# ScalarE in place of VectorE for the two 32-wide casts to bf16 in each expert retrieval

## The chip, the core and the metric

The kernel runs on one core of a Trainium2 chip. The metric is the device time of one execution in microseconds, the median of the runs. TensorE (PE in the rows) multiplies matrices, VectorE is DVE, ScalarE is ACT, GpSimd is POOL and SyncE, which issues most loads, is SP. Each engine works through its own queue in order and waits on semaphores for the others.

## What is computed

One decoder layer over 256 tokens of width 2048: an input projection, a pooling mixer beside sparse attention, an output projection and a layer norm, then the part that matters here, a product-key retrieval over 128 x 128 = 16384 experts with one hidden neuron each, and a second layer norm.

```python
qh = (xc @ wq).reshape(PEER_CHUNK, PEER_HEADS, 2, PEER_HALF)
s1 = jnp.einsum('thd,kd->thk', qh[:, :, 0], sub_keys[0])
s2 = jnp.einsum('thd,kd->thk', qh[:, :, 1], sub_keys[1])
v1, i1 = lax.top_k(s1, PEER_TOPK)          # 16 of 128
v2, i2 = lax.top_k(s2, PEER_TOPK)
cand = (v1[..., :, None] + v2[..., None, :]).reshape(PEER_CHUNK, PEER_HEADS, PEER_TOPK * PEER_TOPK)
cidx = (i1[..., :, None] * PEER_KEYS + i2[..., None, :]).reshape(...)
best, pos = lax.top_k(cand, PEER_TOPK)     # 16 of 256
expert = jnp.take_along_axis(cidx, pos, axis=-1)
gate = jax.nn.softmax(best, axis=-1)
act = jax.nn.gelu(jnp.einsum('td,thkd->thk', xc, u[expert]), approximate=False)
return jnp.einsum('thk,thkd->td', (gate * act), v[expert])
```

## The kernel before

Weights come in units of 128x512 float32 (256 KB). For each unit `load_unit` issues a load into a `raw` buffer (four of them), and `split` makes two halves: `hi` on ScalarE, a cast to the rounded float32 type (L94), and `lo` on VectorE, the difference `raw - hi` (L95), for some units on GpSimd. There are four `hi` and four `lo` buffers. TensorE takes three products for each pair of tiles: hi x hi (L119), lo x hi (L120), hi x lo (L121). So a unit goes through SyncE, ScalarE, VectorE or GpSimd, and TensorE, and a buffer comes free when the last reader is done.

The part around the change has two streams that are woven together. One is the query projection `wq` (48 units here, besides 16 that were loaded early): its result is split into `qhh` and `qhl`, and multiplied with the subkeys into scores `sps`, both halves of a head and both tiles of 128 tokens. Behind it the products `ups` follow, 128 steps of 11 tiles, with units that were loaded ahead into free parts of the large tile `S` (L531). The units u_d are split by the same lines.

The other stream is `retrieve`: 8 heads times 2 token tiles, 16 calls. Each takes the 16 largest of 128 scores for both halves (`top16`: two maxima, two index searches, a replacement on VectorE; `v16` values, `x16` indices). GpSimd adds all pairs into `cand` (L564), VectorE takes the 16 largest of these 256 (`best`, `pos`), takes `pos` apart into `ab` (L571, L572), and compares with 0..15 into the one-hot `hot` (L577). GpSimd multiplies `hot` with the indices (L579), adds up (L582, L583), and VectorE writes the expert number `e_idx` (L584). The two casts of the change stand here: `xb`, the indices `x16` as bf16, which GpSimd's L579 reads, and `abb`, the `ab` pair as bf16, which L577 reads. Both are 128x32.

From `e_idx` GpSimd gathers expert rows with an indirect DMA, `g<-u_g` (L659), which VectorE multiplies and sums (L684). These are spread over the 128 `ups` steps. Then weights are extracted and scattered per token, and the same is done with the `v` table (`vacc`, L805, L813).

The order on each engine is set when the program is built: a scheduler that works with estimated times places the instructions, with a higher priority for what belongs to weight units (`tc.high_priority`). A changed engine can therefore move other instructions too.

Of the kernel before, what the change touches and what calls it, by code (L numbers as in the profile page):

```python
# [71 lines left out]
def layer(ctx, tc, A, out):  # L72
    nc = tc.nc
# [474 lines left out]
    def top16(vals, work, vout, iout):  # L548
        nc.vector.max(vout[:, 0:8], vals)
        nc.vector.max_index(iout[:, 0:8], vout[:, 0:8], vals)  # L550
        nc.vector.match_replace(work, vout[:, 0:8], vals, GONE)
        nc.vector.max(vout[:, 8:16], work)
        nc.vector.max_index(iout[:, 8:16], vout[:, 8:16], work)

    def retrieve(h, tt, sps):
        v16 = wqp.tile([P, 2, PK], F32, name="v16")
        x16 = wqp.tile([P, 2, PK], U32, name="x16")
        for half in range(2):
            vals = sps[:, half * P:(half + 1) * P]
            top16(vals, vals, v16[:, half], x16[:, half])  # L560
        xb = wqp.tile([P, 2, PK], BF16, name="xb", bufs=2)
        nc.vector.tensor_copy(xb, x16)
        cand = wqp.tile([P, PK, PK], F32, name="cand")
        nc.gpsimd.tensor_tensor(cand, v16[:, 0].unsqueeze(2).broadcast_to([P, PK, PK]),  # L564
                                v16[:, 1].unsqueeze(1).broadcast_to([P, PK, PK]), op=ALU.add)
        cflat = cand.rearrange("p a b -> p (a b)")
        pos = wqp.tile([P, PK], U32, name="pos")
        hs_ = slice(h * PK, (h + 1) * PK)
        top16(cflat, cflat, best[:, tt, hs_], pos)
        ab = wqp.tile([P, 2, PK], U32, name="ab")  # L570
        nc.vector.tensor_single_scalar(ab[:, 0], pos, 4, op=ALU.logical_shift_right)  # L571
        nc.vector.tensor_single_scalar(ab[:, 1], pos, 15, op=ALU.bitwise_and)  # L572
        abb = wqp.tile([P, 2, PK], BF16, name="abb", bufs=2)
        nc.vector.tensor_copy(abb, ab)
        hot = wqp.tile([P, PK, 2, PK], BF16, name="hot")
        flat = hot.rearrange("p k a j -> p k (a j)")
        nc.vector.tensor_tensor(hot, iota16.unsqueeze(2).broadcast_to([P, PK, 2, PK]),  # L577
                                abb.unsqueeze(1).broadcast_to([P, PK, 2, PK]), op=ALU.is_equal)
        nc.gpsimd.tensor_tensor(hot, hot, xb.rearrange("p a k -> p k a").unsqueeze(3).broadcast_to([P, PK, 2, PK]),  # L579
                                op=ALU.mult)  # L580
        for n in (8, 4, 2):
            nc.gpsimd.tensor_tensor(flat[:, :n], flat[:, :n], flat[:, n:2 * n], op=ALU.add)  # L582
        nc.gpsimd.tensor_tensor(i12[:, tt, :, hs_], hot[:, 0], hot[:, 1], op=ALU.add)  # L583
        nc.vector.scalar_tensor_tensor(e_idx[:, tt, hs_], i12[:, tt, 0, hs_], float(P), i12[:, tt, 1, hs_],  # L584
                                       op0=ALU.mult, op1=ALU.add)
# [10 lines left out]
    for h in range(HEADS):  # L596
        for half in range(2):
            with tc.high_priority(offset=AHEAD):
                if 2 * h + half < EARLY:
                    ps = first[2 * h + half]  # L600
                else:
                    ps = bankA("wq")[:, :T]
                    rows_T(ps, A["w_q"][2 * h + half], lambda kt: hs[kt])
                for f in late:
                    f()
                qh = tuple(wqp.tile([P, T], F32R, name=f"qh{s}", bufs=2) for s in "hl")
                split(qh[0], qh[1], ps)
            late = [lambda h=h, half=half, qh=qh: scores(h, half, qh)]
        if h == HEADS - 1:
            with tc.high_priority(offset=AHEAD):  # L610
                late[0]()
        if h > 0:
            for tt in range(NT):
                retrieve(h - 1, tt, sps[h - 1][:, tt])
    for tt in range(NT):
        retrieve(HEADS - 1, tt, sps[HEADS - 1][:, tt])
# [337 lines left out]
```

## Time and profile before

| | |
|---|---|
| median of 3 runs | 1751.63 us (1749.29 to 1753.16) |
| profiled execution | 1756.99 us, span from first to last instruction 1755.2 us |
| TensorE busy, granted clock | 1666.4 us (95%), 0.984 |
| VectorE busy | 1450.0 us (83%) |
| ScalarE busy | 897.5 us (51%) |
| GpSimd busy | 886.7 us (51%) |

The busy shares are means over stages that differ. The retrievals lie between 400 and 560 us of the span; the `ups` steps go on to about 1020 us, the extraction to about 1160, and the products with `v` to the end. A row of the trace gives the start of an instruction, its length, and in brackets the idle time of the engine ahead of it with what ended it.

### The profile page before, as it was taken

What the parts mean: (1) busy time and instruction counts of PE and PEld (TensorE: products, weight loads), DVE (VectorE), ACT (ScalarE), POOL (GpSimd) and SP (SyncE); (2) the same over time, 40 slices, a digit from 0 to 9 for tenths busy, and PEclk for the clock granted to TensorE, in tenths of its full rate; (3) what the DMA queues carried; (4) which work ended last, traced back from release to release, by engine and by line L of the source; (5) the groups of instructions that cost most, each with busy time, mean ns of one, the idle gap of its engine ahead of it and who ended that gap; (6) DMA issues with size and microseconds to landing.
All of it is one profiled execution on the core that took longest, in us unless ns stands there. A gap on an engine that the chain in (4) does not pass through costs nothing. (4 is left out here: it accounts for less than half of the span.)

```text
span 1755.2 us, 33099 instructions
## 1 busy us (share of the span) xinstructions
PE 1666.4 (95%) x10652; PEld 1484.7 (85%) x10652; DVE 1450.0 (83%) x3515; ACT 897.5 (51%) x1885; POOL 886.7 (51%) x899
## 2 busy tenths in 40 slices
PE   8999999989899999999999889988999999999996
PEld 8999888869888999999999788876687888888883
DVE  6766676679999888889888798877888888889896
ACT  6545565444344555555554358773454555555551
POOL 0000000036775656566565588856747645456562
PEclk9999999989999999999999999998999999999998
DMA  7667657726688999999999841137999999999962
GB/s 219 179 188 192 203 175 261 255 79 214 193 287 268 337 361 321 323 347 336 344 330 329 293 146 55 55 103 255 296 329 333 381 338 332 338 319 328 352 200 89
DMA packets 206014, 451.13 MB, mean 257 GB/s; under 512 B 26928, under 2 KB 31472, under 8 KB 205328
## 3 DMA queue, kind: packets, MB, share of 16 engines
q1 hardware_dynamic: 164816, 297.93, 51.4%
q0 software_dynamic: 41024, 151.09, 24.7%
q8 instruction: 84, 1.38, 0.3%
q14 instruction: 90, 0.74, 0.1%
HBM read 444.59 MB, written 4.26 MB: 256 GB/s over the span
## 5 line engine op out<-in xcount | busy, mean ns | idle before, releaser
L94 ACT CAST hi<-S 128x512 fp32r<-128x512 f32 x677 | 420.4, 622 | 450.5 <-PE vacc L121 223.2
L95 DVE TENSOR_TENSOR lo<-S,hi 128x512 fp32r<-128x512 f32 x672 | 464.5, 701 | 89.6 <-ACT hi L94 81.4
L121 PE MATMUL ups<-hTh,lo 128*128 128x256 f32 x1408 | 392.2, 283 | 11.7 <-DVE lo L95 11.1
L119 PE MATMUL ups<-hTh,hi 128*128 128x256 f32 x1408 | 392.2, 280 | 4.5 <-ACT hi L94 4.2
L120 PE MATMUL ups<-hTl,hi 128*128 128x256 f32 x1408 | 394.0, 281 | 0.0
L659 POOL DMA_INDIRECT g<-u_g,e_idx x256 | 289.2, 1130 | 173.1 <-DVE g L684 119.4
L94 ACT CAST hi<-raw 128x512 fp32r<-128x512 f32 x327 | 202.0, 621 | 245.4 <-PE projT L120 58.9
L95 DVE TENSOR_TENSOR lo<-raw,hi 128x512 fp32r<-128x512 f32 x303 | 216.6, 720 | 111.3 <-ACT hi L94 107.2
L120 PE MATMUL vacc<-lo,wt 128*128 128x512 f32 x744 | 278.4, 401 | 8.6 <-DVE lo L95 8.5
L121 PEld LDWEIGHTS ups<-hTh,lo 128*128 128x128 f32 x1408 | 263.5, 189 | 16.8 <-DVE lo L95 15.6
L121 PE MATMUL vacc<-hi,wt 128*128 128x512 f32 x744 | 276.2, 399 | 0.0
L119 PEld LDWEIGHTS ups<-hTh,hi 128*128 128x128 f32 x1408 | 266.0, 189 | 6.1 <-ACT hi L94 6.1
L120 PEld LDWEIGHTS ups<-hTl,hi 128*128 128x128 f32 x1408 | 265.7, 189 | 0.0
L119 PE MATMUL vacc<-hi,wt 128*128 128x512 f32 x744 | 231.2, 400 | 7.3 <-ACT wt L94 6.9
L805 POOL DMA_INDIRECT g<-v_g,e_idx x139 | 166.3, 1196 | 128.4 <-DVE accg L813 109.0
L684 DVE SCALAR_TENSOR_TENSOR g<-g,h_gath 128x640 f32<-128x640 f32 x256 | 204.9, 820 | 16.6 <-DMA g<-u_g,e_idx 16.1
L805 POOL DMA_INDIRECT raw<-v_g,e_idx x117 | 137.2, 1173 | 84.7 <-DVE accg L813 65.2
L120 PEld LDWEIGHTS vacc<-lo,wt 128*128 128x128 f32 x744 | 141.1, 190 | 45.7 <-DVE lo L95 12.0
L119 PEld LDWEIGHTS vacc<-hi,wt 128*128 128x128 f32 x744 | 141.2, 190 | 42.9 <-ACT wt L94 8.0
L121 PEld LDWEIGHTS vacc<-hi,wt 128*128 128x128 f32 x744 | 140.9, 189 | 34.5 <-issue 0.5
L714 POOL TENSOR_SCALAR bt<-cst,slotT 128x128 f32<-128x128 f32 x192 | 126.3, 675 | 23.3 <-POOL bt L714 16.4
L294 POOL TENSOR_TENSOR bias<-bias,score 128x128 f32<-128x128 f32 (+1 forms) x16 | 11.5, 739 | 233.1 <-DMA bias<-relb 115.8
(243 smaller groups left out, 3074.1 us busy)
## 6 DMA issues: line engine op xcount, KB each, us to landing
S<-v_d SPq DMA_DIRECT2D x361, 256.0 KB, 5.1
S<-u_d SPq DMA_DIRECT2D x328, 256.0 KB, 5.3
raw<-w_t SPq DMA_DIRECT2D x100, 256.0 KB, 2.8
raw<-w_n SPq DMA_DIRECT2D x64, 256.0 KB, 2.8
raw<-w_o SPq DMA_DIRECT2D x64, 256.0 KB, 3.3
raw<-w_q SPq DMA_DIRECT2D x48, 256.0 KB, 3.1
bc<-i_dram SPq DMA_DIRECT2D x32, 256.0 KB, 3.1
raw<-u_d SPq DMA_DIRECT2D x24, 256.0 KB, 5.1
```

The costliest lines, as they stand in the source:

```text
L94: last_copy[0] = nc.scalar.copy(hi, src).ins
L95: last_split[0] = (eng or nc.vector).tensor_tensor(lo, src, hi.bitcast(F32), op=ALU.subtract).ins
L119: mm(o, l[0], r[0], start=first, stop=False)
L120: mm(o, l[0], r[1], start=False, stop=False)
L121: return mm(o, l[1], r[0], start=False, stop=last).ins
L294: nc.gpsimd.tensor_tensor(bias[:, tt, :n], bias[:, tt, :n], sel[:, tt, :n], op=ALU.add)
L659: nc.gpsimd.indirect_dma_start(out=g, out_offset=None, in_=table, in_offset=bass.IndirectOffsetOnAxis(ap=e_idx[:, tt, slot:slot + 1], axis=0))
L684: nc.vector.scalar_tensor_tensor(g, g, 1.0, h_gath[:, tt], op0=ALU.mult, op1=ALU.mult, accum_out=pd[:, tt, slot:slot + 1])
L714: eng.tensor_scalar(bt[j][:, i], iota, i2T[:, t:t + 1], None, op0=ALU.is_equal)
L805: nc.gpsimd.indirect_dma_start(out=g, out_offset=None, in_=A["v_g"], in_offset=bass.IndirectOffsetOnAxis(ap=e_idx[:, tt, slot:slot + 1], a ...
```

## The change

Both casts of `retrieve` are issued on ScalarE. Nothing else in the text differs.

```diff
         xb = wqp.tile([P, 2, PK], BF16, name="xb", bufs=2)
-        nc.vector.tensor_copy(xb, x16)
+        nc.scalar.copy(xb, x16)
...
         abb = wqp.tile([P, 2, PK], BF16, name="abb", bufs=2)
-        nc.vector.tensor_copy(abb, ab)
+        nc.scalar.copy(abb, ab)
```

The scheduler also places other instructions of this stage anew; in front of it and from the middle of the `ups` steps on, the order is as it was. The sixth of the 16 retrievals shows it. On VectorE, from its `ab` pair on (the numbers tell tiles of one name apart; 5528, 5531 and 5533 belong to this retrieval, `xb_5724`, `cand_5726` and `v16_5747` to the next ones), before and then now:

```order
L571 TENSOR_SCALAR ab_5528<-pos_5522 128x16
L572 TENSOR_SCALAR ab_5528<-pos_5522 128x16
L552 MAX v16_5712<-sps_5460 128x8
L574 CAST abb_5531<-ab_5528 128x32
L553 MAX_INDEX x16_5713<-v16_5712,sps_5460 128x8
L577 TENSOR_TENSOR hot_5533<-iota16_4951,abb_5531 128x512
L562 CAST xb_5724<-x16_5713 128x32
L95 TENSOR_TENSOR lo_6027<-raw_6024,hi_6026 128x512
L549 MAX best_73<-cand_5726 128x8
L549 MAX v16_5747<-sps_5460 128x8
```

```order
L571 TENSOR_SCALAR ab_5528<-pos_5522 128x16
L572 TENSOR_SCALAR ab_5528<-pos_5522 128x16
L552 MAX v16_5712<-sps_5460 128x8
L553 MAX_INDEX x16_5713<-v16_5712,sps_5460 128x8
L584 SCALAR_TENSOR_TENSOR e_idx_72<-i12_74 128x16
L577 TENSOR_TENSOR hot_5533<-iota16_4951,abb_5531 128x512
L549 MAX best_73<-cand_5726 128x8
L549 MAX v16_5747<-sps_5460 128x8
L550 MAX_INDEX pos_5728<-best_73,cand_5726 128x8
L550 MAX_INDEX x16_5748<-v16_5747,sps_5460 128x8
L551 MATCH_REPLACE sps_5460<-v16_5747,sps_5460 128x128
L95 TENSOR_TENSOR lo_6027<-raw_6024,hi_6026 128x512
```

The two casts are gone, `e_idx` of an earlier retrieval stands ahead of `hot`, and `lo_6027` has moved behind two maxima, two index searches and a replacement. On ScalarE, at the same place, before and now:

```order
L94 CAST hi_5907<-raw_5905 128x512
L94 CAST hi_5926<-raw_5924 128x512
L94 CAST hi_6026<-raw_6024 128x512
L94 CAST qhh_5863<-wq_5782 128x256
L94 CAST hi_6045<-raw_6043 128x512
L94 CAST hi_6063<-raw_6061 128x512
L94 CAST hi_6082<-raw_6080 128x512
```

```order
L94 CAST hi_5907<-raw_5905 128x512
L574 CAST abb_5531<-ab_5528 128x32
L94 CAST hi_5926<-raw_5924 128x512
L562 CAST xb_5724<-x16_5713 128x32
L94 CAST hi_6026<-raw_6024 128x512
L94 CAST qhh_5863<-wq_5782 128x256
L94 CAST hi_6045<-raw_6043 128x512
L94 CAST hi_6063<-raw_6061 128x512
L574 CAST abb_5737<-ab_5734 128x32
L94 CAST hi_6082<-raw_6080 128x512
```

The `hi` casts keep their order among themselves, and `hi_5926`, `hi_6026` and `hi_6082` now stand behind casts that wait for VectorE. On GpSimd, at the same place, before and now:

```order
L564 TENSOR_TENSOR cand_5726<-v16_5712 128x256
L95 TENSOR_TENSOR lo_5927<-raw_5924,hi_5926 128x512
L579 TENSOR_TENSOR hot_5533<-hot_5533,xb_5518 128x512
L95 TENSOR_TENSOR lo_6046<-raw_6043,hi_6045 128x512
L582 TENSOR_TENSOR hot_5533<-hot_5533 128x256
```

```order
L564 TENSOR_TENSOR cand_5726<-v16_5712 128x256
L579 TENSOR_TENSOR hot_5533<-hot_5533,xb_5518 128x512
L95 TENSOR_TENSOR lo_5927<-raw_5924,hi_5926 128x512
L582 TENSOR_TENSOR hot_5533<-hot_5533 128x256
L95 TENSOR_TENSOR lo_6046<-raw_6043,hi_6045 128x512
```

Both `lo` of GpSimd have moved one place back, behind a step of the one-hot work.

## Rows read from the trace of the kernel before

**Rows 1.** The page: busy time, share of the span and instructions of each engine.
```profile
PE 1666.4 (95%) x10652; PEld 1484.7 (85%) x10652; DVE 1450.0 (83%) x3515; ACT 897.5 (51%) x1885; POOL 886.7 (51%) x899
```
**Rows 2.** Busy time by stage; columns as in the first line.
```profile
core 0: us, PE busy (x) PEld busy (x) DVE busy (x) ACT busy (x) POOL busy (x), PEclk, DMA share, GB/s
400.00:480.00 80.00, 73.31 (x587) 71.88 (x586) 77.98 (x301) 29.21 (x54) 57.93 (x68) 0.96 0.64 206
480.00:560.00 80.00, 72.64 (x577) 69.68 (x575) 78.60 (x271) 36.34 (x69) 54.35 (x67) 0.98 0.83 275
...
580.00:960.00 380.00, 380.00 (x3227) 379.84 (x3226) 332.53 (x691) 196.44 (x364) 237.81 (x210) 1.00 0.96 338
```
**Rows 3.** Waits of TensorE, 400 to 580 us: total, times, longest.
```profile
PE ups L121 <- DVE lo L95: 6.3, 9, 2.6
PE wq L121 <- DVE lo L95: 5.3, 5, 1.9
```
**Rows 4.** Groups by shape on VectorE, 400 to 570 us: busy us, mean ns.
```profile
L562 DVE CAST xb<-x 128x32 bf16<-128x32 uint32 x16 | 12.1, 754 | 0.1
...
L553 DVE FIND_INDEX8 x<-v,sps 128x8 uint32<-128x128 f32 x32 | 9.1, 284 | 0.0
...
L574 DVE CAST abb<-ab 128x32 bf16<-128x32 uint32 x16 | 4.3, 272 | 0.0
```
**Rows 5.** VectorE in order of time, sixth retrieval: start us, length us.
```profile
455.10 0.16 DVE L572 TENSOR_SCALAR ab<-pos 128x16 uint32<-128x16 uint32 x1
455.18 0.29 DVE L552 MAX8 v<-sps 128x8 f32<-128x128 f32 x1
455.39 0.16 DVE L574 CAST abb<-ab 128x32 bf16<-128x32 uint32 x1
...
455.78 0.66 DVE L577 TENSOR_TENSOR hot<-iota,abb 128x512 bf16<-128x512 bf16 x1
456.37 1.26 DVE L562 CAST xb<-x 128x32 bf16<-128x32 uint32 x1
```
**Rows 6.** GpSimd in order of time, the same place.
```profile
456.12 1.47 POOL L95 TENSOR_TENSOR lo<-raw,hi 128x512 fp32r<-128x512 f32 x1
```
**Rows 7.** VectorE in order of time, first retrieval.
```profile
406.48 0.16 DVE L562 CAST xb<-x 128x32 bf16<-128x32 uint32 x1
406.55 0.28 DVE L549 MAX8 v<-sps 128x8 f32<-128x128 f32 x1
```
**Rows 8.** Groups by shape on ScalarE, first the whole span, then 400 to 570 us.
```profile
L733 ACT ACTIVATE val<-val 128x8 f32<-128x8 f32 x32 | 6.4, 200 | 8.1 <-DVE val L732 8.1
...
L629 ACT ACTIVATE best<-best 128x128 f32<-128x128 f32 x2 | 0.6, 312 | 3.0 <-DVE best L627 3.0
```
**Rows 9.** ScalarE in order of time: `hi` at the first, eighth and last retrieval.
```profile
411.93 0.62 ACT L94 CAST hi<-raw 128x512 fp32r<-128x512 f32 x1 [0.22 <-DVE sps L551]
...
468.50 0.62 ACT L94 CAST hi<-raw 128x512 fp32r<-128x512 f32 x1 [2.62 <-PE wq L120]
...
544.91 0.62 ACT L94 CAST hi<-S 128x512 fp32r<-128x512 f32 x1 [0.78 <-DMA S<-u_d]
```
**Rows 10.** VectorE: end of the `ab` pair in these three, and the last `e_idx`.
```profile
413.05 0.16 DVE L572 TENSOR_SCALAR ab<-pos 128x16 uint32<-128x16 uint32 x1
...
473.57 0.16 DVE L572 TENSOR_SCALAR ab<-pos 128x16 uint32<-128x16 uint32 x1
...
550.17 0.17 DVE L572 TENSOR_SCALAR ab<-pos 128x16 uint32<-128x16 uint32 x1
...
556.24 0.17 DVE L584 SCALAR_TENSOR_TENSOR e_idx<-i 128x16 int32<-128x16 f32 x1 [1.03 <-POOL i L583]
```
**Rows 11.** Waits of ScalarE, 400 to 560 us.
```profile
ACT hi L94 <- DMA raw<-w_q: 27.7, 17, 3.7
```

## The prediction

> **What bounds the kernel now.** I began with the busy shares of the page: TensorE is busy for 95% of the span, VectorE for 83%, ScalarE for 51% [rows 1]. A change on VectorE and ScalarE can therefore only pay where TensorE is not the limit, so the next view is the busy time by stage. The retrievals fall into 400 to 560 us. There the reader should see two things. First, VectorE is full: 77.98 and 78.60 us of two stretches of 80 us. Second, TensorE does 587 and 577 matrix products in them, 1164 in 160 us, while from 580 to 960 us it does 3227 in 380 us and is never idle [rows 2]. At that later pace, 380/3227 = 0.118 us each, 1164 products need 137 us. So TensorE loses about 23 us in this stage, and at 580 us it is back at full pace with nothing made up. The third view says on whom it waits: on the `lo` halves of the weights that VectorE subtracts, 6.3 + 5.3 = 11.6 us of idle time in 14 waits [rows 3]. (Idle time is less than lost time here, because matrix products that come late also come thinly spaced.) The stage is VectorE's, and a microsecond freed there can reach TensorE, up to some 12 to 23 us. What follows is TensorE at full pace to 960 us, so a shift at 560 us travels on to there. I expect it to travel to the end, because every later load and gather is released by work in step with TensorE.
>
> **What the change removes.** The two casts take 12.1 us (16 `xb`, mean 754 ns) and 4.3 us (16 `abb`, mean 272 ns) of VectorE [rows 4], together 16.4 us. Not all of that is freed. A short instruction overlaps its neighbour: the `ab` shift at 455.10 is followed by the next start at 455.18, and the `xb` at 406.48 by a start at 406.55 [rows 5, 7]. So an undisturbed cast, 0.16 us long, holds up the queue for 0.08 us. Thirty-two of them free 32 x 0.08 = 2.6 us for certain. The rest of the 16.4 us is 16.4 - 32 x 0.16 = 11.3 us by which casts are stretched. Where that comes from is seen in one place: `xb` starts at 456.37 and lasts 1.26 us, until 457.63 [rows 5], while GpSimd runs its `lo` from 456.12 to 457.59 [rows 6]. The cast stands until GpSimd's instruction is over. `FIND_INDEX8` meets the same GpSimd work and has the same length everywhere, 284 ns in the mean of 32 [rows 4], so not every VectorE instruction is held like this.
>
> How much of the 11.3 us is really saved depends on who comes next. In the new order the instructions behind `hot` are two maxima, two index searches and a replacement, and only then a `lo`. The searches are not held. But GpSimd was busy for 57.93 us of 80 [rows 2], so the next instruction that can be held (`lo`, `hot`, the `ab` pair, `e_idx`) will often meet another GpSimd instruction. Also, the GpSimd `lo` that `xb` used to wait for now stands behind GpSimd's `hot`, so it falls closer to VectorE's own `lo`. The bounds are nothing saved and all saved. Nothing in the trace tells which is nearer, and I take half, 5.7 us. VectorE is then freed of 2.6 + 5.7 = 8.3 us, with bounds of 2.6 and 13.9.
>
> **What it adds.** ScalarE gets 32 casts of 128x32. The trace has none there. The nearest rows are an activation of 128x8 at 200 ns and one of 128x128 at 312 ns [rows 8]; I take 0.22 us, nearest the first, and 32 x 0.22 = 7 us on an engine that is busy for 29.21 us of 80 [rows 2]. That time alone costs nothing.
>
> The hand-over can cost. `hot` on VectorE needs `abb`. In the old order one maximum and one index search stood around the cast; in the new order they stand between the `ab` pair and `hot`, sometimes with `e_idx` or a `lo` as well. From the end of the pair (455.26) to the start of `hot` (455.78) that is about 0.5 us, the cast's own share of 0.1 included [rows 5], so 0.4 us of cover against 0.22. If ScalarE is free when the pair ends, `hot` does not wait. If a `hi` cast has just begun, 0.62 us long [rows 9], the hop takes up to 0.84 and `hot` waits up to 0.4 us. With ScalarE busy for a third of the time, this is about 16 x 0.33 x 0.2 = 1 us in all. I charge 1 us, with bounds of 0 and 16 x 0.4 = 6.4.
>
> The `xb` that is cast at this point serves GpSimd's product of the next retrieval (5533 is multiplied with `xb_5518`, cast one retrieval earlier), about 9 us later, so its hop costs nothing. Without that lead GpSimd would wait some 0.3 us each time, and it has 22 us of idle time in 80.
>
> The queue behind the casts is the second thing. ScalarE works in order, and its `hi` casts ran ahead of VectorE. Where a `hi` starts before the `ab` pair is done, the cast in front of it now makes it wait. I went through the 16 places, taking the end of the second `ab` [rows 10] less the start of the ScalarE instruction that will stand behind `abb` [rows 9]. The first is 413.21 - 411.93 = 1.3 us, the eighth 473.73 - 468.50 = 5.2, the last 550.34 - 544.91 = 5.4; two are nothing, and the 16 add up to 42 us. Most of this should not be felt: four `hi` buffers lie between ScalarE and TensorE, these `hi` halves then waited for their `lo` anyway, and VectorE comes to the pair sooner than it did. I take nothing, and price the other case below.
>
> The sum: 8.3 - 1 = 7.3 us freed on VectorE, less than the 11.6 and the 23 us that TensorE can take up, and some of TensorE's thin spacing should go too, which I round up to **8 us**. The profiled execution took 1756.99 us around its span of 1755.2; the sum makes it 1749. The median of the unprofiled runs is 5.4 us lower, 1751.63, and becomes **1743.6**.
>
> A page speaks against this. The Trainium skill, in "VectorE: DVE Perf Modes", section on the TRN2 errata, has a table of fixed costs in which a copy of 32 elements between SBUF places is (58 + 32)/0.96 GHz = 94 ns on VectorE and (224 + 32)/1.2 GHz = 213 ns on ScalarE. "ScalarE: Activation LUTs", in its rules for kernel authors, gives simple arithmetic to VectorE. By that table alone 32 casts get 3.8 us dearer and the estimate would be 1755.4. The undisturbed casts of this trace agree in kind (0.16 us long, 0.08 in the queue), but the mean of `xb` is 754 ns.
>
> **The rivals.**
> *The cast was cheap, and the wait moves on.* If the next VectorE instruction stands behind the same GpSimd work each time, only the 2.6 us of the short casts are freed, and `hot`'s hand-over takes as much (16 x 0.16 us, something between my 1 us and the bound of 6.4). The sum is 0, and the time 1751.6. For it: GpSimd's 72% busy share, and `lo` moved to where it meets VectorE's `lo`. Against it: two or more unheld instructions stand behind `hot` now. This is how the Trainium skill's table would come true.
> *ScalarE falls into step with VectorE.* The place is a `hi` held behind `abb` or `xb`, whose `lo` GpSimd makes: its raw buffer comes free late, the next `w_q` load starts late, and ScalarE already waits 27.7 us for these loads [rows 11]. A retrieval takes (550.34 - 413.21)/15 = 9.14 us, and TensorE needs 4 units of 12 products and 6 score products, 54 x 0.118 = 6.4 us. The point from which it decides is thus a hold of 2.7 us. Seven of the 16 holds are longer, by 12.3 us together. All of that lost, against 8 gained, is +4.3, and the time 1755.9. Against it: the holds are counted from VectorE's old, late times, and late ones belong to `lo` halves that VectorE now makes behind the pair anyway.
>
> **How the numbers follow.** The forecast has 0.63; its own range comes from VectorE's bounds, -(13.9 - 0) to -(2.6 + 0.3 x 11.3 - 2), where a third of the stretching is saved and 2 us are lost at `hot`: 1737.7 to 1747.6. "The wait moves on" has 0.20, because the busy GpSimd is a real obstacle. The slower rival has 0.17. About 0.2% (3.5 us) is what a measurement here can tell from no change. All of the forecast but 0.05 is faster by more than that, and 0.02 of the first rival: 0.60. Of the second rival 0.13 is slower by more, and 0.03 of the first: 0.16. The rest is 0.24. The range 1736 to 1756 takes in the forecast's own range and both rivals' times, and leaves out about 0.13: what goes beyond my best case for VectorE, and holds that cost more than counted.
>
> **What would show it.** Right: between 400 and 560 us the TensorE count rises well above 1164 and the idle time before `lo` falls below 11.6 us; the last `e_idx` of the retrievals comes 6 to 10 us sooner than 556.24 [rows 10]; VectorE's `lo` and `ab` means rise, but by less than 11.3 us in all; 580 to 960 us looks the same, earlier. Wrong in the first way: `lo`, `ab` and `hot` take up the whole stretching. Wrong in the second: ScalarE's idle time before `hi` is ended by VectorE, TensorE waits for GpSimd's `lo`, and w_q loads land late. A gain at 560 us that is gone at 1020 would refute the step that a shift travels on, and a GpSimd or ScalarE wait at `hot` above 2 us the charge for the hand-over.

## The result, and the profile after

The changed kernel took 1744.86 us, the median of 11 runs (1736.69 to 1746.80). The kernel before took 1751.79 us in 11 runs on the same chip (1748.54 to 1757.03). The recorded ratio of the two sets of runs is 0.995, with a 95% interval of 0.9937 to 0.9962. The medians differ by 6.9 us, which by itself is a ratio of 0.996. The change is faster, by about 0.4 to 0.5%. The forecast was 1743.6.

The profiled execution of after took 1739.89 us, its span 1738.1. That is among the fastest of its 11 runs, while the profile of before was at the slow end of its own. The two profiles differ by 17.1 us and the medians by 6.9, so the profiles are compared here by what happens inside the stage of the retrievals, and the totals by medians. The first part of the page, to be held against [rows 1]:

```profile
PE 1657.5 (95%) x10652; PEld 1477.1 (85%) x10652; DVE 1434.8 (83%) x3483; ACT 899.2 (52%) x1917; POOL 884.1 (51%) x899
```

VectorE has 32 instructions and 15.2 us less, ScalarE 32 instructions more. The busy time by stage of after, columns as in [rows 2]:

```profile
400.00:480.00 80.00, 74.36 (x605) 72.62 (x604) 76.59 (x308) 31.73 (x75) 63.90 (x74) 0.98 0.71 222
480.00:560.00 80.00, 75.54 (x615) 72.64 (x614) 75.95 (x250) 39.51 (x87) 59.71 (x69) 1.00 0.86 286
560.00:580.00 20.00, 19.93 (x168) 19.76 (x169) 18.38 (x40) 9.98 (x19) 13.49 (x13) 1.00 0.91 306
580.00:960.00 380.00, 378.68 (x3245) 378.48 (x3245) 333.58 (x696) 198.00 (x369) 233.97 (x209) 1.00 0.96 339
```

TensorE does 605 + 615 = 1220 products between 400 and 560 us, 56 more than the 1164 of before. With the next 20 us, where before had 155, it is 1388 against 1319. Those 69 products are 69 x 0.118 = 8.1 us of TensorE's later pace. From 580 to 960 us the pace is as it was. VectorE is no longer quite full: 76.59 and 75.95 us against 77.98 and 78.60.

TensorE's waits from 400 to 580 us (total, times, longest), against [rows 3], and the last `e_idx`, against [rows 10]:

```profile
PE wq L121 <- DVE lo L95: 4.7, 4, 1.7
PE ups L121 <- DVE lo L95: 3.0, 6, 1.0
...
547.84 0.18 DVE L584 SCALAR_TENSOR_TENSOR e_idx<-i 128x16 int32<-128x16 f32 x1 [1.03 <-POOL i L583]
```

The idle time before `lo` falls from 11.6 to 7.7 us, and the retrievals end at 547.84 where they ended at 556.24: 8.4 us sooner.

Those 3.9 us of idle time are half of the 8.1 us that TensorE won. Much of the rest is its clock, which the sections above leave out. These rows of before show TensorE at the end of a wait, then a stretch that follows and the one behind it (columns as in [rows 2]):

```profile
467.14 0.39 PE L121 MATMUL wq<-hTh,lo 128*128 128x256 f32 x1 [1.90 <-DVE lo L95]
...
468.50:471.90 3.40, 3.40 (x18) 3.40 (x17) 3.40 (x13) 1.51 (x3) 2.57 (x5) 0.50 0.62 222
471.90:475.30 3.40, 3.40 (x31) 3.40 (x30) 3.40 (x19) 1.24 (x2) 0.62 (x1) 1.00 0.70 217
```

TensorE is busy throughout both. At a granted clock of 0.50 (1.2 GHz) it does 18 products in 3.4 us, at 1.00 (2.4 GHz) it does 31. Before has three stretches of 3.4 us at 0.50 between 400 and 560 us (from 444.6, 468.5 and 492.4), after has one (from 473.0). Each of the four begins at the end of one of TensorE's longest waits in this stage, or up to 1.4 us later (1.84, 1.90 and 2.63 us long in before, 1.63 in after); another wait of 1.67 us in after is not followed by one. Two stretches less are, as an estimate from these rows, 2 x 13 = 26 products, or 26 x 0.118 = 3.1 us.

**Where VectorE got the time from.** These are VectorE's other groups by shape from 400 to 560 us, busy us and mean ns of one. First before, which the sections above did not show:

```profile
L95 DVE TENSOR_TENSOR lo<-S,hi 128x512 fp32r<-128x512 f32 x36 | 27.8, 774 | 0.0
L95 DVE TENSOR_TENSOR lo<-raw,hi 128x512 fp32r<-128x512 f32 x22 | 20.6, 937 | 0.3 <-ACT hi L94 0.3
L577 DVE TENSOR_TENSOR hot<-iota,abb 128x512 bf16<-128x512 bf16 x16 | 7.8, 489 | 0.0
L571 DVE TENSOR_SCALAR ab<-pos 128x16 uint32<-128x16 uint32 x16 | 7.6, 472 | 0.0
L572 DVE TENSOR_SCALAR ab<-pos 128x16 uint32<-128x16 uint32 x16 | 4.3, 271 | 0.0
L584 DVE SCALAR_TENSOR_TENSOR e_idx<-i 128x16 int32<-128x16 f32 x16 | 4.0, 250 | 1.0 <-POOL i L583 1.0
```

And after:

```profile
L95 DVE TENSOR_TENSOR lo<-S,hi 128x512 fp32r<-128x512 f32 x41 | 34.7, 853 | 0.5 <-ACT hi L94 0.4
L95 DVE TENSOR_TENSOR lo<-raw,hi 128x512 fp32r<-128x512 f32 x23 | 20.5, 891 | 1.5 <-ACT hi L94 1.5
L577 DVE TENSOR_TENSOR hot<-iota,abb 128x512 bf16<-128x512 bf16 x16 | 8.2, 514 | 0.1
L584 DVE SCALAR_TENSOR_TENSOR e_idx<-i 128x16 int32<-128x16 f32 x16 | 8.0, 502 | 2.3 <-POOL i L583 2.2
L571 DVE TENSOR_SCALAR ab<-pos 128x16 uint32<-128x16 uint32 x16 | 3.1, 197 | 0.0
L572 DVE TENSOR_SCALAR ab<-pos 128x16 uint32<-128x16 uint32 x16 | 2.7, 171 | 0.0
```

I take lengths near the shortest of the trace as undisturbed (`lo` 0.67 us, `hot` 0.41, the small ones 0.16) and call what a mean lies above that, times its count, the stretching. Before, with the casts of [rows 4], it is 30.4 us; after, 20.5. The casts' own 11.3 us are gone. The `ab` pair lost 6.0 us of stretching too, which nobody had asked for. `e_idx` took up 4.0 us, `lo` 3.0, `hot` 0.4: -11.3 - 6.0 + 4.0 + 3.0 + 0.4 = -9.9. Add 2.6 us for the 32 short casts, and 12.5 us are freed. VectorE's idle time in these 160 us rose from 3.4 to 7.5 us, so 12.5 - 4.1 = 8.4 us should show at the end of the stage. That the last `e_idx` shows just this is partly luck. The window of after holds some work of the next stage, and its retrievals began later (first maximum at 402.70 us, in before at 401.75). From the first maximum to the end of the last `e_idx` the stage is 154.7 us long before and 145.3 after, 9.3 us shorter. VectorE's waits of after (400 to 580 us) name the new idle time. None of them is at `hot`:

```profile
DVE e_idx L584 <- POOL i L583: 2.2, 3, 1.0
DVE lo L95 <- ACT hi L94: 2.1, 5, 1.1
...
DVE best L549 <- POOL cand L564: 1.2, 4, 0.5
```

Before, these were 1.0, 0.3 and 0.2 us.

**The sixth retrieval again.** VectorE, then GpSimd, then ScalarE in order of time (start, length), after, against [rows 5, 6]:

```profile
452.81 0.16 DVE L572 TENSOR_SCALAR ab<-pos 128x16 uint32<-128x16 uint32 x1
...
453.49 0.41 DVE L584 SCALAR_TENSOR_TENSOR e_idx<-i 128x16 int32<-128x16 f32 x1
453.83 0.41 DVE L577 TENSOR_TENSOR hot<-iota,abb 128x512 bf16<-128x512 bf16 x1
...
455.61 1.65 DVE L95 TENSOR_TENSOR lo<-raw,hi 128x512 fp32r<-128x512 f32 x1
```
```profile
453.25 0.62 POOL L564 TENSOR_TENSOR cand<-v 128x256 f32<-128x256 f32 x1
...
455.44 1.26 POOL L95 TENSOR_TENSOR lo<-raw,hi 128x512 fp32r<-128x512 f32 x1
```
```profile
453.01 0.22 ACT L574 CAST abb<-ab 128x32 bf16<-128x32 uint32 x1 [4.22 <-DVE ab L572]
453.13 0.61 ACT L94 CAST hi<-raw 128x512 fp32r<-128x512 f32 x1
453.67 0.22 ACT L562 CAST xb<-x 128x32 bf16<-128x32 uint32 x1
```

ScalarE's cast ends at 453.23, 0.6 us before `hot` starts: the hand-over is hidden. `hot` lasts 0.41 us where it lasted 0.66. The price has moved to two others. `e_idx` stands from 453.49 to 453.90, until GpSimd's `cand` (to 453.87) is over. `lo` meets GpSimd's `lo`, which ends at 456.70, and takes 1.65 us where one alone takes 0.67: it ends at 457.26, 0.56 us after GpSimd's.

### The profile page after: what moved, and what is told of

It reads as the page before. It is cut to its first block, busy times and chain, and to the rows that moved or that the text cites. A ratio compares the mean times of both kernels' runs of the same rounds, so it can differ in the third digit from the quotient of the medians.

```text
span 1738.1 us, 33114 instructions
## 1 busy us (share of the span) xinstructions
PE 1657.5 (95%) x10652; PEld 1477.1 (85%) x10652; DVE 1434.8 (83%) x3483; ACT 899.2 (52%) x1917; POOL 884.1 (51%) x899
## 5 line engine op out<-in xcount | busy, mean ns | idle before, releaser
L659 POOL DMA_INDIRECT g<-u_g,e_idx x256 | 284.8, 1112 | 171.4 <-DVE g L684 124.2
L805 POOL DMA_INDIRECT g<-v_g,e_idx x139 | 161.3, 1161 | 127.0 <-DVE accg L813 107.2
```

Source lines behind the costliest of these rows:

```text
L659: nc.gpsimd.indirect_dma_start(out=g, out_offset=None, in_=table, in_offset=bass.IndirectOffsetOnAxis(ap=e_idx[:, tt, slot:slot + 1], axis=0))
L805: nc.gpsimd.indirect_dma_start(out=g, out_offset=None, in_=A["v_g"], in_offset=bass.IndirectOffsetOnAxis(ap=e_idx[:, tt, slot:slot + 1], a ...
```

## The experiments

Three batches ran, each beside runs of before on the same chip; the medians of before there were 1765.68 us (30 runs), 1761.62 (23) and 1751.82 (35). Only ratios are therefore compared across batches. The first batch splits the change.

**One cast alone.** `xb_only` moves only L562, `abb_only` only L574.

```diff
-        nc.vector.tensor_copy(xb, x16)
+        nc.scalar.copy(xb, x16)
```

> Only xb is cast on ScalarE; abb stays on VectorE. Theory A (VectorE is freed of what the casts hold up its queue, mostly the time in which they are stretched beside GpSimd): xb carries about 10.8 of the 13.8 us, so the last e_idx of the retrievals, at 556.24 us before and 547.84 with both casts moved, comes near 549.7, and the time is about 5 us below before. Theory B (the scheduler's new order of the other instructions makes the gain, whichever cast is moved): one cast moved gives as much as two or as little as none, without regard to its share. Theory C (the cast was cheap, the wait passes to the next VectorE instruction): the means of lo, ab and e_idx on VectorE rise by what xb gave up, and the time is within 2 us of before.

Measured: 1761.75 us, ratio 0.998 (0.9966 to 0.9994), last `e_idx` at 551.2, 1207 products from 400 to 560 us. That is between what theory A and theory C gave, and near A. Its order of the later stages changed as well, so its total is a weaker witness than its stage. And behind the stage, from 566.5 to 573.3 us, TensorE's granted clock is 0.50: by 580 us it has done 1317 products, no more than before's 1319.

```diff
-        nc.vector.tensor_copy(abb, ab)
+        nc.scalar.copy(abb, ab)
```

> Only abb is cast on ScalarE; xb stays on VectorE. Theory A: abb carries 1.3 us of queue time and 1.8 us of stretching, less the hop in front of hot, so the last e_idx comes near 554.5 and the time is 0 to 2 us below before; xb on VectorE keeps a mean near 750 ns. Theory B: as large a gain as with both, 7 us. Theory C: no change, and hot waits for ScalarE.

Measured: 1756.55 us, ratio 0.9957 (0.994 to 0.9975), last `e_idx` at 549.5, 1215 products. Groups of VectorE, 400 to 560 us:

```profile
L562 DVE CAST xb<-x 128x32 bf16<-128x32 uint32 x16 | 7.9, 492 | 0.2
...
L572 DVE TENSOR_SCALAR ab<-pos 128x16 uint32<-128x16 uint32 x16 | 5.5, 343 | 0.0
```

The cast that was 1.8 us of stretching brings the stage's end 6.7 us forward, most of the gain. Theory A had asked for 554.5 and an `xb` near 750 ns, so it failed here, and the result is near that of theory B. `xb`, still on VectorE, fell from 754 to 492 ns, and the stretching in all from 30.4 to 21.9 us. So the casts' shares do not add up: what a cast costs depends on where it and GpSimd's work stand, and the scheduler placed both anew.

**The casts on GpSimd.** Both go to `nc.gpsimd.tensor_copy`.

```diff
-        nc.vector.tensor_copy(xb, x16)
+        nc.gpsimd.tensor_copy(xb, x16)
...
-        nc.vector.tensor_copy(abb, ab)
+        nc.gpsimd.tensor_copy(abb, ab)
```

> Both casts go to GpSimd in place of ScalarE. Theory A: VectorE is freed of the same instructions, so it gains as well, but GpSimd, busy for 64 us of 80, gets 32 casts of some 0.25 us more (8 us), which can hold VectorE's instructions in their turn: last e_idx between 548 and 553, time 2 to 6 us below before. Theory D (it is ScalarE's idle time that matters, since an engine that is nearly full itself passes the load back): no gain or a loss, up to 5 us above before.

Measured: 1761.92 us, ratio 0.9976 (0.996 to 0.9991), last `e_idx` at 552.5, 1217 products, stretching 20.4 us. That lies within theory A. It frees VectorE as ScalarE does, and still ends the stage later: the casts take 459 and 477 ns each on GpSimd, where 250 were expected, and GpSimd waits 10.2 us for the `ab` pair. Here too the later stages are in another order.

**VectorE's load put back.** The changed kernel, and VectorE makes the two casts as well, into tiles that nobody reads.

```diff
         nc.scalar.copy(xb, x16)
+        spx = wqp.tile([P, 2, PK], BF16, name="spx", bufs=2)
+        nc.vector.tensor_copy(spx, x16)
...
         nc.scalar.copy(abb, ab)
+        spa = wqp.tile([P, 2, PK], BF16, name="spa", bufs=2)
+        nc.vector.tensor_copy(spa, ab)
```

> As changed, with both casts on ScalarE, and two casts of the same size into tiles that nothing reads put back on VectorE in each retrieval. Theory A: VectorE has its old load again and the hop over ScalarE on top: last e_idx at 555 to 558, time back at that of before, within 3 us. Theory B (the hand-over to ScalarE and the order that it brings make the gain): the time stays some 7 us below before.

Measured: 1761.91 us, ratio 0.9979 (0.9963 to 0.9995), last `e_idx` at 550.7, 1208 products, stretching 23.8 us. Behind the stage its order is that of after and before.

```profile
L564 DVE CAST spx<-x 128x32 bf16<-128x32 uint32 x16 | 9.2, 576 | 0.1
...
L578 DVE CAST spa<-ab 128x32 bf16<-128x32 uint32 x16 | 2.8, 172 | 0.0
```

Neither theory came out: A had the end at 555 to 558 us, B the whole gain. With its load back, VectorE loses 550.7 - 547.8 = 2.9 us of the 8.4, and the total about half of its gain. The other 5.5 us stay. They cannot come from the work that left VectorE, since it has not left; they come with the new arrangement, in which nothing on VectorE's path waits for those casts and the instructions stand elsewhere beside GpSimd's. Its ledger against before says where: the stretching of the two casts is 6.9 us in place of 11.3, of the `ab` pair 4.6 in place of 6.8, of `lo` 7.4 in place of 9.6, while `hot` rises from 1.3 to 3.3 and `e_idx` from 1.4 to 1.6. That is 6.6 us less in all, with the same instructions on VectorE.

**Repeats, and ScalarE loaded more.** The second batch took before and after again, on another chip.

> The kernel before, profiled once more beside the others of this call, since the four runs so far were on a chip on which the kernel before takes 1765.7 us. If the first profile is typical, TensorE does 1164 +- 10 products from 400 to 560 us, the last e_idx is at 555 to 557 us, and xb on VectorE has a mean near 750 ns. If it is not, the count is near 1205, as in the variants, and the earlier comparison of single profiles was misleading.

Measured: 1759.53 us in a single run, last `e_idx` at 556.1, 1163 products, stretching 30.4 us.

> The changed kernel once more, timed. Theory A: 5 to 9 us faster than before on this chip too, last e_idx 7 to 9 us ahead of before_again. Theory E (the gain of the stage is given back where the next weight units land late): TensorE does fewer than 150 products from 560 to 580 us, and the gain is 2 to 5 us.

Measured: 1754.24 us (12 runs), ratio 0.9951 (0.9932 to 0.9971), last `e_idx` at 548.1, 1219 products, stretching 20.8 us. So the stage repeats on another chip, to 0.3 us. The last `S` copy of the `ups` steps comes at 1015.9 us against 1024.2, 8.3 us sooner, and the last `val` at 1164.4 against 1171.7, 7.3 sooner.

```diff
         nc.scalar.copy(xb, x16)
+        for i in range(2):
+            spare = wqp.tile([P, 2, PK], BF16, name="spare", bufs=2)
+            nc.scalar.copy(spare, x16)
```

> As changed, with two more casts of x16 on ScalarE in each retrieval into tiles that nothing reads (32 more, 7 us of ScalarE). Theory A: ScalarE has this time to spare, so the result is that of the changed kernel within 2 us. Theory F (ScalarE's queue is what limits the gain: hi casts held behind small ones): 3 to 6 us slower than the changed kernel, and TensorE waits for hi.

Measured: 1752.97 us, ratio 0.995 (0.9928 to 0.9972), last `e_idx` at 547.9. The group on ScalarE, 400 to 570 us:

```profile
L565 ACT CAST spare<-x 128x32 bf16<-128x32 uint32 x32 | 5.5, 214 | 0.4 <-DVE x L553 0.4
```

32 more casts, 5.5 us, cost nothing: ScalarE's own time in this stage is free.

**GpSimd makes no `lo`.** The kernel before with all `lo` halves on VectorE.

```diff
-POOL_U = (1, 3)
-POOL_UU = (1,)
+POOL_U = ()
+POOL_UU = ()
```

> The kernel before, with the casts on VectorE, but GpSimd makes no lo: VectorE makes them all. It asks what stretches the casts. If it is GpSimd's work beside them, the mean of xb falls from 754 ns to 300 to 450 (cand and hot remain), and lo on raw from 937 to below 800. If the casts are long for a reason of their own, the means stay. VectorE gets some 28 lo more (19 us), so the kernel is about 10 to 18 us slower than before.

Measured: 1789.45 us in a single run, 27.8 us above the median of before where 10 to 18 were expected; last `e_idx` at 569.8, stretching 18.3 us. The `ab` pair fell to 164 ns and `lo` from `raw` from 937 to 752 ns, but `xb` only to 670. I had taken GpSimd's `lo` for the holder of `xb`, and that was too narrow. VectorE, then GpSimd, in order of time there:

```profile
426.46 1.08 DVE L562 CAST xb<-x 128x32 bf16<-128x32 uint32 x1
```
```profile
426.08 1.42 POOL L579 TENSOR_TENSOR hot<-hot,xb 128x512 bf16<-128x512 bf16 x1 [0.43 <-DVE hot L577]
```

`xb` now stands until 427.54, GpSimd's product of the one-hot until 427.50. I then compared each stretched cast (over 0.25 us) with GpSimd's rows. In this kernel all 16 end 0.03 to 0.05 us after an instruction of GpSimd, be it L579 or `cand` (L564). In the kernel before 13 of 15 do by the rows; the other two end inside a row that groups two additions of GpSimd, and in the trace's single records they too end 0.04 us after the first of the two. So `lo`, `cand`, the one-hot product and the additions (L582) all held casts that met them.

**Is it the bf16 output?** The kernel before, with `xb` written as float32. All five engines keep the order of before.

```diff
-        xb = wqp.tile([P, 2, PK], BF16, name="xb", bufs=2)
+        xb = wqp.tile([P, 2, PK], F32, name="xb", bufs=2)
```

> The kernel before, with the xb cast written as float32 instead of bf16 and still on VectorE; the order of all instructions on all engines is that of before, only GpSimd's product with the indices reads another type. Theory A, a cast that meets a GpSimd instruction stands until that ends, whatever it writes: mean of xb 650 to 850 ns, last e_idx 555 to 557.5, ratio 0.998 to 1.002. Rival B, the hold belongs to the bf16 output: mean of xb below 300 ns. Then the same order with some 8 us of stretching less tells whether stretching alone is worth time: last e_idx 548 to 552 if it is, 555 or later if the next lo takes it up.

Measured: 1750.34 us, ratio 0.9995 (0.9979 to 1.001). The last `e_idx` is at 558.3, 0.8 us outside what theory A gave, in a profiled execution whose retrievals also began late (first maximum at 403.4, in before at 401.75). VectorE's group, then the sixth `xb`, then GpSimd's `lo` beside it:

```profile
L562 DVE CAST xb<-x 128x32 f32<-128x32 uint32 x16 | 12.2, 764 | 0.1
```
```profile
458.36 1.26 DVE L562 CAST xb<-x 128x32 f32<-128x32 uint32 x1
```
```profile
458.11 1.47 POOL L95 TENSOR_TENSOR lo<-raw,hi 128x512 fp32r<-128x512 f32 x1
```

It is 764 ns against 754, and the hold is the same to 0.01 us as in [rows 5, 6]. The output's type is not its cause; rival B falls.

**The arrangement alone.** The kernel before with the `xb` lines written ahead of L579.

```diff
-        xb = wqp.tile([P, 2, PK], BF16, name="xb", bufs=2)
-        nc.vector.tensor_copy(xb, x16)
...
+        xb = wqp.tile([P, 2, PK], BF16, name="xb", bufs=2)
+        nc.vector.tensor_copy(xb, x16)
         nc.gpsimd.tensor_tensor(hot, hot, xb.rearrange("p a k -> p k a").unsqueeze(3).broadcast_to([P, PK, 2, PK]),
```

> The kernel before, both casts on VectorE, the xb cast written behind the one-hot comparison in the text, so that it stands in another place of VectorE's queue and the scheduler places its neighbours anew. Theory C, the new arrangement carries much of the gain: VectorE's stretching in 400 to 560 us falls from 30 to 20 to 25 us, last e_idx 549 to 553, ratio 0.995 to 0.998. Rival A, only what leaves VectorE pays: stretching 28 to 32 us, last e_idx 555 or later, ratio 0.999 to 1.004 (more, if GpSimd's product now waits for xb).

Measured: 1750.0 us, ratio 0.9988 (0.9974 to 1.0003), last `e_idx` at 557.3, stretching 30.6 us. The numbers are those of rival A, but the run does not decide: the scheduler gave VectorE, ScalarE and GpSimd exactly the order of before, so this is before once more. Whether the new arrangement pays with both casts needed from VectorE stays untested.

**One more instruction off VectorE.** The changed kernel, and `e_idx` leaves VectorE too.

```diff
-        nc.vector.scalar_tensor_tensor(e_idx[:, tt, hs_], i12[:, tt, 0, hs_], float(P), i12[:, tt, 1, hs_],
-                                       op0=ALU.mult, op1=ALU.add)
+        i1s = wqp.tile([P, PK], F32, name="i1s", bufs=2)
+        nc.gpsimd.tensor_single_scalar(i1s, i12[:, tt, 0, hs_], float(P), op=ALU.mult)
+        nc.gpsimd.tensor_tensor(i1s, i1s, i12[:, tt, 1, hs_], op=ALU.add)
+        nc.scalar.copy(e_idx[:, tt, hs_], i1s)
```

> The changed kernel, and e_idx too leaves VectorE: GpSimd scales and adds (two instructions of 128x16), ScalarE casts to int32. VectorE is freed of 8.0 us of e_idx and 2.2 us of waits for it. Theory, VectorE still sets the stage's end in the changed kernel: the retrievals' last index 3 to 7 us sooner than 548, some 1220 products grow to 1240 to 1270 in 400 to 560 us, ratio to before 0.990 to 0.9935. Rival 1, GpSimd's extra 6 us stretch VectorE's other instructions by as much: last index 546 to 550, ratio 0.994 to 0.996. Rival 2, the longer hand-over to the gathers or ScalarE's longer queue costs: ratio above 0.9965.

> The changed kernel once more, on the chip of these runs: ratio 0.993 to 0.9965, last e_idx 547 to 549.

Measured: 1745.17 us, ratio 0.997 (0.9954 to 0.9985), beside the changed kernel's 1745.65 us, ratio 0.9959 (0.9943 to 0.9974). It is no faster. Of the expectations, the theory (3 to 7 us sooner, 1240 to 1270 products) failed; the last `e_idx` lies where rival 1 had it and the ratio where rival 2 had it. Its busy time by stage:

```profile
400.00:480.00 80.00, 76.50 (x630) 74.13 (x628) 73.91 (x298) 34.58 (x84) 68.14 (x88) 1.00 0.73 226
480.00:560.00 80.00, 73.78 (x602) 71.33 (x603) 74.31 (x242) 38.89 (x95) 63.97 (x85) 1.00 0.83 281
```

VectorE is freed of 4 us more (73.91 + 74.31 against 76.68 + 75.63 in the changed kernel of that batch), and stretching is down to 17.3 us. TensorE gets 13 products from it by 560 us and 4 by 580. The last `e_idx`, now on ScalarE, comes at 549.7, later than 547.8, and VectorE waits 4.5 us for `cand` where it waited 1.2. So VectorE is no longer alone in setting this stage's end; that the waits for GpSimd and the hand-overs take its place is the likely reading, which no run isolates. Its later stages are in another order too, so the last 0.1% is not to be read from its total.

In the same batch the profile of the changed kernel, beside that of `xb_f32` (which has the order of before), shows how the shift travels. The rows are of each kernel's source lines: lengths in ns, then start of the first and of the last. First `xb_f32`:

```profile
L584 DVE SCALAR_TENSOR_TENSOR e_idx<-i x16: 151/162/1106, 421.5 to 558.3; 128x16 int32<-128x16 f32 x16
...
L680 ACT COPY S<-ups x128: 379/389/427, 503.5 to 1018.3; 128x256 f32<-128x256 f32 x128
...
L733 ACT ACTIVATE val<-val x32: 192/198/213, 1027.4 to 1166.1; 128x8 f32<-128x8 f32 x32
```

And the changed kernel:

```profile
L584 DVE SCALAR_TENSOR_TENSOR e_idx<-i x16: 152/411/1242, 420.4 to 547.8; 128x16 int32<-128x16 f32 x16
...
L680 ACT COPY S<-ups x128: 377/389/398, 494.7 to 1009.0; 128x256 f32<-128x256 f32 x128
...
L733 ACT ACTIVATE val<-val x32: 191/198/209, 1018.2 to 1156.6; 128x8 f32<-128x8 f32 x32
```

10.5, 9.3 and 9.5 us: what is won at 560 is still there at 1160.

All of them in one table. Stretching is counted as above; products are TensorE's from 400 to 560 us.

| kernel | last `e_idx` | products | stretching, us | ratio to before |
|---|---|---|---|---|
| before, again | 556.2, 556.1 | 1164, 1163 | 30.4, 30.4 | 1 |
| xb_f32 | 558.3 | 1166 | 30.2 | 0.9995 |
| late_xb (order of before) | 557.3 | 1171 | 30.6 | 0.9988 |
| gpsimd_casts | 552.5 | 1217 | 20.4 | 0.9976 |
| xb_only | 551.2 | 1207 | 22.4 | 0.998 |
| dve_load_back | 550.7 | 1208 | 23.8 | 0.9979 |
| abb_only | 549.5 | 1215 | 21.9 | 0.9957 |
| after, again, third | 547.8, 548.1, 547.8 | 1220, 1219, 1219 | 20.5, 20.8, 20.6 | 0.995, 0.9951, 0.9959 |
| scalar_tripled | 547.9 | 1217 | 21.2 | 0.995 |
| e_idx_moved | 549.7 | 1232 | 17.3 | 0.997 |
| no_pool_lo | 569.8 | 1252 | 18.3 | single run |

Every arrangement that differs from before has 17 to 24 us of stretching where before has 30. TensorE's clock goes the same way: in 400 to 560 us the kernels with the order of before have 10.2 to 13.7 us at a granted clock of 0.50, all others 0 to 3.4. So the column of products holds more than VectorE's time.

## Why the prediction was right

*The stage is VectorE's, and what is freed there reaches TensorE.* Right, and shown three times: 8.4, 8.0 and about 10 us at the last `e_idx`, and 66 to 69 products more by 580 us in the three pairs of profiles. The idle time before `lo` fell by 3.9 us only. The prediction put what goes beyond idle time down to products that come thinly spaced. For some 3.1 of the 8.1 us the rows show another cause, a term that it does not have: TensorE's granted clock was 0.50 for 3.4 us in place of 10.2. The same holds for the 23 us that it counted as lost: about 3 x 13 = 39 products, 4.6 us, were lost in those three stretches.

*A shift travels on to the end.* Right as far as 1160 us. From there to the end single executions differ by more than the shift: on the second chip 7.3 us at the last `val` were 1.3 us at the end of the span, in the first pair 12.4 were 17.1. In the first pair TensorE's clock goes along with that: from 1160 us to 20 us before the end of the span the granted clock was 0.50 for 17.0 us in before and 3.4 in after. The medians say 6.9, 7.4 and 6.2 us.

*The short casts free 2.6 us for certain.* Putting the casts back cost 2.9 us of the stage. That fits, but those casts were stretched as well, by 6.9 us, so it is not a clean measure of this term.

*Half of the stretching is saved, 5.7 us.* The direction was right, the size too small, and the picture behind it too simple. The stretching fell by 9.9 us, not 5.7. The prediction counted what would come back on others and did not think that an instruction which stays could lose stretching. The `ab` pair did, by 6.0 us: in before, five holds of the pair that end with a GpSimd `lo` (those of 411.85, 446.66, 462.85, 489.68 and 500.35 us) make 5.9 of its 6.8 us, and in the new order none is left. How much of the stretching falls on the pair changes from one execution to the next (3.7 us in `before_again`, where the sum is 30.4 all the same; 0.8 in all three of the changed kernel), so 6.0 is the upper end of some 3 to 6. What was given back, 4.0 us on `e_idx`, 3.0 on `lo` and 0.4 on `hot`, is less than 11.3, as foretold, but the `ab` means fell where they were to rise, and so did that of `lo` from `raw` (937 to 891 ns).

*The hand-over costs 1 us at `hot`.* The place was wrong: `hot` waited 0.1 us. The charge came up elsewhere: 4.1 us of idle time that VectorE did not have before, in front of `e_idx`, `lo` and the maxima of `cand`. So 9.9 for 5.7 and 4.1 for 1 nearly cancel: 2.6 + 9.9 - 4.1 = 8.4 against the 7.3 summed and the 8 forecast. The direction was understood; that the forecast time came within 1.3 us of the measured one is luck in these two terms.

*ScalarE's casts are free, and the `hi` held behind them are not felt.* Each cast took 218 and 217 ns, forecast 0.22 us. ScalarE's waits of after, 400 to 560 us:

```profile
ACT abb L574 <- DVE ab L572: 34.6, 13, 4.3
ACT hi L94 <- DMA raw<-w_q: 12.9, 9, 3.7
```

The holds are real, 34.6 us in 13 waits where 42 in 14 were counted. ScalarE waited 14.8 us less for its loads in exchange [rows 11], and TensorE's waits for GpSimd's `lo` stayed below 1 us. So the condition of the rival "ScalarE falls into step with VectorE" came about, and its price did not.

*"The cast was cheap, and the wait moves on"* had a part of the truth: 7.4 us of stretching did move to `e_idx`, `lo` and `hot`. It fell because more than that vanished. With it falls what the Trainium skill's table ("VectorE: DVE Perf Modes", the section on the TRN2 errata) would have made of the time, 1755.4: its 213 ns for ScalarE agree with the 217 and 218 measured, its 94 ns for VectorE lie near the 0.08 us of queue of an undisturbed cast, but casts beside a busy GpSimd took 754 ns.

So the mechanism is wider than the prediction had it. About a third of the stage's gain (2.9 of 8.4 us) is the load that left VectorE. The other 5.5 us came with `dve_load_back`'s arrangement, in which VectorE's instructions meet GpSimd's less (6.6 us less stretching). What stays open is whether such an arrangement needs the casts to be off VectorE's path: no run had a new arrangement with both casts needed from VectorE.

## What to carry to other kernels

Where GpSimd is busy, look at the means by shape on VectorE: a small instruction far above its shortest length is being held, and its cost is its place beside GpSimd rather than its work. Moving two such instructions to an idle engine freed more than their floor here, but the scheduler's new order decided how much; read the whole ledger of stretching and new waits, and measure the parts, since they do not add up. Where TensorE waits, read its granted clock as well as its idle time: what it does at the lower clock (18 products in place of 31 in 3.4 us here) is lost time that no wait shows. When the freed engine is no longer the only one that ends the stage, the next instruction moved off it can bring nothing, as `e_idx` did here.

## What the runs showed of the hardware that was not expected

- A cast of 128x32 on VectorE takes 0.16 us alone. One that meets an instruction of GpSimd stands until that ends, and ends 0.03 to 0.05 us later: all 15 stretched casts in before (13 by the rows, two by the trace's single records), 16 of 16 in no_pool_lo. `lo`, `hot` and `cand` of GpSimd all did this, and the cast's output type (bf16 754 ns, float32 764) made no difference. `FIND_INDEX8` kept its length beside the same work (284 ns over 128 scores, 406 to 420 over 256 of `cand`). The Trainium skill ("GPSIMD Engine Reference", section 1, Specifications) says that GpSimd shares its SBUF interfaces with VectorE, in contention with VectorE instructions that have two SBUF inputs or run in a 2-port mode. The trace agrees as far as it goes: the stretched `lo`, `hot` and `e_idx` have two inputs in SBUF, and `qhl`, one of whose two lies in PSUM in this kernel, kept its length (394 to 424 ns). The search names two tiles in its row, but its eight values have a row of their own ahead of it (`MATCH_VALUE_LOAD`), so it may read only one. In which mode the casts run, no row shows.
- Longer instructions of VectorE are held in the same way and then still take most of their own time. Between 400 and 560 us all 20 `lo` of before that took more than 0.72 us, and all 25 of after, end 0.54 to 0.56 us after the end of a GpSimd instruction (the one at 455.61 takes 1.65 us); `hot` ends 0.28 us after, 6 of 6 and 3 of 3; `e_idx` 0.03 to 0.04 us after. What is left after GpSimd's end is thus the undisturbed length (0.67, 0.41, 0.16 us) less 0.12 to 0.13 us.
- TensorE did 18 products in 3.4 us at a granted clock of 0.50 and 31 at 1.00; four such stretches at 0.50 in this stage (three in before, one in after) began as a wait of 1.6 to 2.6 us ended or up to 1.4 us later.
- The same 128x32 cast takes 217 ns on ScalarE and 459 to 477 ns on GpSimd.
